# A transformer encoder layer on one core: the first stage written out in engine order, and half of a side product moved into it

## The chip, the cores and the metric

The kernel runs on one core of a Trainium2 chip. A core has five engines that each work through a list of instructions of their own, in order: TensorE (PE, matrix products; its weight loads are listed as PEld), VectorE (DVE), ScalarE (ACT), GpSimd (POOL) and SyncE (SP), which issues most of the transfers between the main memory and the core's own memory. They wait for one another through semaphores only. The metric is the device time of one execution in microseconds (us). Lower is better.

## The reference, cut to what matters

The layer normalizes 512 tokens of width 1024, projects them, runs two kinds of attention, adds a mixture of experts and a gated per-layer embedding. What the change touches:

```
h = layer_norm(x, emb_ln_g, emb_ln_b)                  # x: 512 x 1024
z = h @ w_in                                           # columns: NA q | NA k | NA v | c_q | c_kv | k_r
...
gate = jax.nn.sigmoid(h @ ple_gate_w[i] + ple_gate_b[i])
ple = gate * (p[i] @ ple_w[i])                         # p[i]: 512 x 256, ple_w[i]: 256 x 1024
```

`p[i] @ ple_w[i]` needs none of the layer's results, so it can be computed at any time before the gate.

## The kernel before, in words

Tokens are cut into four chunks of 128 (`h[0]` to `h[3]`, a chunk is 128 partitions x 1024). Most products are done in split precision: a float32 operand is cut into a high part (`...h`, a cast on ScalarE, line 94) and the remainder (`...l`, a subtraction on VectorE, line 95) by `split`, and `mm3` issues three products, high x high (L109), high x low (L110) and low x high (L111). Where operands are plain float32, one `nc.tensor.matmul` does the product.

**The first stage** (lines 260 to 279) is the program up to `v_na`, the NA v columns of `z`. For each chunk c, `layer_norm` runs on VectorE: two `bn_stats` of half a row each, `bn_aggr`, the variance plus epsilon `ve`; a square root `sd` on ScalarE; then `(h - mu) * eg`, five operations on 128 x 1 (the reciprocal, and `rsqrt_refine`), and `h * y + eb`. `eg` and `eb` are gain and bias, read once for each of the 128 partitions (`row_bcast`). `transpose_to` transposes the chunk on TensorE (eight 128 x 128 pieces into two `tr` tiles of PSUM) and splits the two tiles into `hTh`, `hTl`. Then eight steps of `mm3` (24 products of 128 x 512) sum up `pj`, and ScalarE copies it to `v_na`. The weight, columns 1024 to 1535 of `w_in`, comes in four pieces `raw` that are split into `aTh`, `aTl`. After the first stage come the latent projections (`latent_k`, weights by `in_cols`, columns from 1920), the attention, the output projection and the second normalization.

In this first stage the order of the instructions is not that of the code: the scheduler of the language orders each engine's list by its own estimates. The attention after it stands under `tc.manual_schedule` for TensorE, which keeps the order as written.

**The place of the side product** (lines 594 to 619) is after the attention. `pT` and `ple_w` are split, and for each of two halves hf of the columns and each chunk c, two steps of `mm3` (six products of 128 x 512) go to a tile `mm`, ScalarE copies it (`p_exp`, L618), and SP stores it to `ple_dram` (L619). It is read back much later, from line 986. The scheduler places these products among the normalizations `layer_norm(h[c], lg, lb, ...)` and transposes of the same stage. The routing projection with `w_q` follows (tiles `mm<-hTh,whi`, L109 to L111): its first two weights are each used in two passes of 256 tokens.

Of the kernel before, what the change touches and what calls it, by code (L numbers as in the profile page):

```python
# [9 lines left out]
F32 = mybir.dt.float32  # L10
# [5 lines left out]
OP = mybir.AluOpType  # L16
# [3 lines left out]
D = 1024  # L20
T = 512
# [49 lines left out]
def tile_encoder_layer(ctx: ExitStack, tc: tile.TileContext, A: dict, out: bass.AP):  # L71
# [97 lines left out]
    def ps_tile(name, bufs=2):  # L169
        return ps6.tile([128, 512], F32, name=name, bufs=bufs)  # L170
# [46 lines left out]
    def run_heads(kinds, feeds, at_unit):  # L217
# [32 lines left out]
        while step():  # L250
            pass

    aw = pA.enter_context(tc.tile_pool(name="aw", bufs=2, reuse_waits="tile"))
    p1 = ExitStack()
    iv = p1.enter_context(tc.tile_pool(name="iv", bufs=1, reuse_waits="tile"))
# [1 line left out]

    with tc.tile_pool(name="ln0", bufs=1, reuse_waits="tile") as ln0:  # L260
        nc.sync.dma_start(h[0], A["x"][0:128, :])
        eg = row_bcast(ln0, A["emb_ln_g"], "eg")
        eb = row_bcast(ln0, A["emb_ln_b"], "eb")
        for c in range(1, 4):
            nc.sync.dma_start(h[c], A["x"][c * 128:(c + 1) * 128, :])
        for c in range(4):
            layer_norm(h[c], eg, eb)
            transpose_to(hTh, hTl, h[c], c)
            if c == 0:
                for kk in range(4):  # L270
                    raw = wst.tile([128, 2, 512], F32, name="raw", bufs=3)
                    nc.sync.dma_start(raw, A["w_in"][kk * 256:(kk + 1) * 256, 1024:1536].rearrange(
                        "(k p) n -> p k n", p=128))
                    split(aTh[:, 2 * kk:2 * kk + 2], aTl[:, 2 * kk:2 * kk + 2], raw)
            cs = slice(c * 128, (c + 1) * 128)
            ps = ps_tile("pj")
            for k in range(8):
                mm3(ps, (hTh[:, k, cs], hTl[:, k, cs]), (aTh[:, k], aTl[:, k]), k == 0, k == 7)
            nc.scalar.copy(v_na[:, c, :], ps)

    ip = p1.enter_context(tc.tile_pool(name="ip", bufs=2, reuse_waits="tile"))
    v_sh = ip.tile([128, 3, 512], F32, name="v_sh", bufs=1)
# [7 lines left out]
    def in_cols(src, c0, ncols):  # L290

        return stream(src[:, c0:c0 + ncols].rearrange("(k p) n -> p k n", p=128), [8, ncols])

    def proj_steps(ps, w, m=128):
        for k in range(8):
# [10 lines left out]
    nc.sync.dma_start(gk, A["kg"])  # L306

    def latent_k(i, lat):
        w = in_cols(A["w_in"], 1920 + i * 128, 128)
# [279 lines left out]
    for c in range(4):  # L589
# [6 lines left out]
    ple_w = [stream(A["ple_w"][:, hf * 512:(hf + 1) * 512].rearrange("(k p) n -> p k n", p=128), [2, 512], scale=0.5)  # L596
             for hf in range(2)]
    for c in range(4):
        cs = slice(c * 128, (c + 1) * 128)
        ps = ps_tile("pj")  # L600
# [5 lines left out]
        transpose_to(hTh, hTl, h[c], c)  # L606


    for hf in range(2):
        hs = slice(hf * 512, (hf + 1) * 512)  # L610
        w = ple_w[hf]
        for c in range(4):
            cs = slice(c * 128, (c + 1) * 128)
            ps = ps_tile("mm")
            for k in range(2):
                mm3(ps, (pTh[:, k, cs], pTl[:, k, cs]), (w[0][:, k], w[1][:, k]), k == 0, k == 1)
            pl = aw.tile([128, 512], F32, name="p_exp", bufs=4)
            nc.scalar.copy(pl, ps)  # L618
            nc.sync.dma_start(ple_dram[c, :, hs], pl)  # L619
    p3.close()  # L620
    pA.close()

# [758 lines left out]
```

## Time and profile before

| what | value |
|---|---|
| three runs | 1562.61 to 1564.3 us, median 1564.05 us |
| the profiled execution, its own time | 1563.9 us |
| its span, from the first to the last instruction | 1562.1 us |
| PE busy | 1495.0 us (96%) |
| DVE busy | 1294.7 us (83%) |
| ACT busy | 647.3 us (41%) |
| transfers | 460.37 MB, mean 295 GB/s |

The share of busy time is a mean over the whole execution. The change touches the first 50 us and some 15 us around 310 us, so these two places are read by themselves, with the rows shown below.

### The profile page before, as it was taken

How to read it: one execution, taken by the hardware profiler on the slowest of the kernel's cores; microseconds unless marked ns; L12 is line 12 of the kernel's file. 1: busy time of each engine (PE TensorE's matmuls, PEld its weight loads, DVE VectorE, ACT ScalarE, POOL GpSimd, SP SyncE). 2: the span in 40 equal slices, each digit the busy share in tenths (PEclk: the TensorE clock that was granted, in tenths of full speed). 3: DMA queues.
4: the chain of work that ended last, by engine and by line, in shares of the span. 5: the costliest groups of instructions: out<-in, count | busy, mean ns of one | idle time of the engine just before them, and what ended most of it. 6: DMA issues, size and time to landing. Idle time of an engine off the chain costs nothing.

```text
span 1562.1 us, 22502 instructions
## 1 busy us (share of the span) xinstructions
PE 1495.0 (96%) x7715; PEld 1267.5 (81%) x7715; DVE 1294.7 (83%) x2895; ACT 647.3 (41%) x1171; POOL 559.6 (36%) x521
## 2 busy tenths in 40 slices
PE   6999899999999999999999989999899999999996
PEld 4788777788887889789888977888688888888885
DVE  7376795779989898988889938898688999998998
ACT  3265685333222566157424513333333333333332
POOL 1023110020015333443323346666434556655460
PEclk9999999999999999999999999999999999999998
DMA  7242341172239999999989999999999999999992
GB/s 232 64 115 80 90 122 42 57 257 81 73 130 356 326 390 391 397 409 419 416 316 374 388 386 354 403 398 392 361 397 377 377 398 397 401 395 398 382 335 110
DMA packets 189857, 460.37 MB, mean 295 GB/s; under 512 B 16560, under 2 KB 80432, under 8 KB 186672
## 3 DMA queue, kind: packets, MB, share of 16 engines
q1 hardware_dynamic: 121552, 213.55, 38.3%
q0 software_dynamic: 58400, 208.69, 35.2%
q10 hardware_dynamic: 9792, 36.70, 5.8%
q8 instruction: 61, 1.00, 0.3%
q14 instruction: 52, 0.43, 0.1%
HBM read 415.11 MB, written 40.89 MB: 292 GB/s over the span
## 4 chain that ended last, share of the span: by engine, by line
PE 70%; DMA 13%; DVE 12%; issue 3%; ACT 1%; POOL 0%; SPq 0%; ACTq 0%; DVEq 0%; POOLq 0%
PE acc L111 10%; PE acc L110 10%; PE acc L109 9%; PE mm L949 6%; PE hp L949 4%; DMA raw<-in_uT_dram 3%; PE mm L109 3%; PE tr L843 3%; PE mm L111 3%; PE pj L109 3%; PE mm L110 3%; PE pj L110 3%; PE pj L111 3%; DMA whi<-in_u_rows_dram,s_ix 3%; DMA wlo<-in_u_rows_dram,s_ix 2%
## 5 line engine op out<-in xcount | busy, mean ns | idle before, releaser
L949 PE MATMUL mm<-whole,raw 128*128 128x256 f32 x1120 | 252.0, 381 | 5.4 <-DMA raw<-in_uT_dram 4.9
L1167 POOL DMA_INDIRECT gat<-in_v_rows_dram,i_sel x128 | 194.4, 1519 | 154.3 <-DVE base L1169 124.8
L949 PEld LDWEIGHTS mm<-whole,raw 128*128 128x128 f32 x1120 | 209.8, 191 | 35.5 <-issue 4.4
L1152 POOL DMA_INDIRECT gat<-in_u_rows_dram,i_sel x97 | 147.1, 1516 | 110.6 <-DVE gat L1158 86.8
L109 PE MATMUL acc<-v_hi,a_hi 128*128 128x512 f32 x456 | 178.6, 392 | 6.1 <-ACT v_hi L94 6.1
L110 PE MATMUL acc<-v_lo,a_hi 128*128 128x512 f32 x456 | 178.7, 392 | 0.5 <-DVE v_lo L95 0.5
L111 PE MATMUL acc<-v_hi,a_lo 128*128 128x512 f32 x456 | 178.9, 393 | 0.1
L94 ACT CAST whi<-raw 128x1024 fp32r<-128x1024 f32 (+4 forms) x119 | 119.3, 1003 | 142.6 <-PE mm L110 41.0
L95 DVE TENSOR_TENSOR wlo<-raw,whi 128x1024 fp32r<-128x1024 f32 (+4 forms) x119 | 138.6, 1165 | 46.9 <-ACT whi L94 46.0
L1169 DVE SCALAR_TENSOR_TENSOR base<-gat,hdot,base 128x1024 f32<-128x1024 f32 x128 | 164.9, 1288 | 1.7
L94 ACT CAST v_hi<-v_raw 128x1024 fp32r<-128x1024 f32 x76 | 79.9, 1052 | 174.0 <-issue 88.7
L95 DVE TENSOR_TENSOR v_lo<-v_raw,v_hi 128x1024 fp32r<-128x1024 f32 x76 | 92.7, 1220 | 37.1 <-ACT v_hi L94 36.9
L110 PE MATMUL acc<-wlo,a_hi 128*128 128x512 f32 x312 | 121.6, 390 | 0.4 <-DVE wlo L95 0.4
L111 PE MATMUL acc<-whi,a_lo 128*128 128x512 f32 x312 | 121.5, 389 | 0.0
L1158 DVE SCALAR_TENSOR_TENSOR gat<-gat,h 128x1024 f32<-128x1024 f32 x97 | 114.7, 1222 | 8.1 <-DMA gat<-in_u_rows_dram,i_sel 8.1
L109 PE MATMUL acc<-whi,a_hi 128*128 128x512 f32 x312 | 121.3, 390 | 0.0
L894 POOL DMA_INDIRECT whi<-in_u_rows_dram,s_ix x43 | 44.9, 1044 | 211.2 <-DVE cand L747 133.1
L877 DVE TENSOR_SCALAR oh_j<-iota,eT 128x128 f32<-128x128 f32 x384 | 116.8, 379 | 0.0
L109 PEld LDWEIGHTS acc<-v_hi,a_hi 128*128 128x128 f32 x456 | 86.2, 189 | 23.9 <-ACT v_hi L94 6.6
L111 PEld LDWEIGHTS acc<-v_hi,a_lo 128*128 128x128 f32 x456 | 86.0, 189 | 18.8 <-DVE a_lo L95 1.0
L110 PEld LDWEIGHTS acc<-v_lo,a_hi 128*128 128x128 f32 x456 | 86.1, 189 | 18.5 <-DVE v_lo L95 1.0
L843 PEld LDWEIGHTS tr<-oh_i,oh_j 128*128 128x128 f32 x768 | 94.2, 193 | 7.7 <-ACT g_st L854 2.5
(364 smaller groups left out, 3355.4 us busy)
## 6 DMA issues: line engine op xcount, KB each, us to landing
raw<-in_uT_dram SPq DMA_DIRECT2D x116, 512.0 KB, 7.8
v_raw<-in_v_rows_dram SPq DMA_DIRECT2D x78, 512.0 KB, 12.9
raw<-in_v_rows_dram SPq DMA_DIRECT2D x50, 512.0 KB, 11.8
g_dram<-g_st ACTq DMA_DIRECT2D x24, 1024.0 KB, 8.8
ge_dram<-ge ACTq DMA_DIRECT2D x44, 256.0 KB, 7.2
ge<-ge_dram SPq DMA_DIRECT2D x44, 256.0 KB, 12.8
g_wide<-g_dram SPq DMA_DIRECT2D x9, 1024.0 KB, 17.9
raw<-in_w_in_dram SPq DMA_DIRECT2D x17, 512.0 KB, 4.0
```

Source lines behind the costliest of these rows:

```text
L94: nc.scalar.copy(hi, src)
L95: nc.vector.tensor_tensor(lo, src, r32(hi), op=OP.subtract)
L109: nc.tensor.matmul(ps, a[0], b[0], start=start, stop=False)
L110: nc.tensor.matmul(ps, a[0], b[1], start=False, stop=False)
L111: nc.tensor.matmul(ps, a[1], b[0], start=False, stop=stop)
L843: nc.tensor.matmul(ps[:, i * 128:(i + 1) * 128], oj[:, 4 * r + i, :], oi[:, 4 * r + i, :], start=True, stop=True)
L877: nc.vector.tensor_scalar(oj[:, i], iota, eT[:, 1, t0 + i:t0 + i + 1], eT[:, 2, t0 + i:t0 + i + 1], op0=OP.is_equal, op1=OP.mult)
L949: nc.tensor.matmul(ps[:, :N_U], raw[:, k], whole[:, k, :], start=(k == 0), stop=(k == 7))
L1152: nc.gpsimd.indirect_dma_start(out=u[:], out_offset=None, in_=u_rows, in_offset=bass.IndirectOffsetOnAxis(ap=i_sel[:, c, k:k + 1], axis=0))
L1158: nc.vector.scalar_tensor_tensor(u, u, 1.0, h[c], op0=OP.mult, op1=OP.mult, accum_out=hdot[:, c, k:k + 1])
L1167: nc.gpsimd.indirect_dma_start(out=u[:], out_offset=None, in_=v_rows, in_offset=bass.IndirectOffsetOnAxis(ap=i_sel[:, c, k:k + 1], axis=0))
L1169: nc.vector.scalar_tensor_tensor(base[c], u, hdot[:, c, k:k + 1], base[c], op0=OP.mult, op1=OP.add)
```

## The change

It has four parts.

1. The first stage stands under `tc.manual_schedule` for TensorE, VectorE and ScalarE: each of these lists now has the order in which the code emits. The pieces are generators that the code steps by hand (`norm_steps` in three parts, `v_steps` in eight steps and a copy).
2. The bias `eb` is no longer read once per partition. One row `b_row` is read, and two products with a column of ones (contraction over one partition) spread it over the partitions; ScalarE copies them.
3. The loads stand in the order of their use. The first latent weight `w_k` is loaded and split inside the first stage.
4. The first half (columns 0 to 511) of the side product is computed in the first stage, in plain float32: `ple_early`, two products of 128 x 512 for each chunk, a scaling copy on ScalarE, a store issued by GpSimd. At the old place only the second half is left.

```diff
-    with tc.tile_pool(name="ln0", bufs=1, reuse_waits="tile") as ln0:
+    with tc.tile_pool(name="ln0", bufs=1, reuse_waits="tile") as ln0, tc.manual_schedule(
+            engines={nc.tensor.engine, nc.vector.engine, nc.scalar.engine}):
         nc.sync.dma_start(h[0], A["x"][0:128, :])
+        b_row = ln0.tile([1, D], F32, name="b_row")
+        nc.sync.dma_start(b_row, ...)
         eg = row_bcast(ln0, A["emb_ln_g"], "eg")
-        eb = row_bcast(ln0, A["emb_ln_b"], "eb")
-        for c in range(1, 4):
+        eb = ln0.tile([128, D], F32, name="eb")
+        p_in = ln0.tile([128, 2, T], F32, name="p_in")
+        nc.sync.dma_start(p_in, A["pT"].rearrange("(k p) t -> p k t", p=128))
+        w_in0 = ln0.tile([128, 2, 512], F32, name="w_in0")
+        nc.sync.dma_start(w_in0, A["ple_w"][:, 0:512].rearrange("(k p) n -> p k n", p=128))
+        vraw = []
+        for kk in range(4):
+            vraw.append(...)
+            nc.sync.dma_start(vraw[kk], A["w_in"][kk * 256:(kk + 1) * 256, 1024:1536].rearrange(
+                "(k p) n -> p k n", p=128))
+            if kk == 2:
+                nc.sync.dma_start(h[1], A["x"][128:256, :])
+        for c in (2, 3):
             nc.sync.dma_start(h[c], A["x"][c * 128:(c + 1) * 128, :])
-        for c in range(4):
-            layer_norm(h[c], eg, eb)
-            transpose_to(hTh, hTl, h[c], c)
...
+        def norm_steps(r):
...
+            nc.scalar.sqrt(sd, ve)
+            yield
+            nc.vector.scalar_tensor_tensor(r, r, mu[:, 0:1], eg, op0=OP.subtract, op1=OP.mult)
...
+            rsqrt_refine(y, y0, ve, t)
+            yield
+            nc.vector.scalar_tensor_tensor(r, r, y, eb, op0=OP.mult, op1=OP.add)
+            yield
+        def ple_early(c):
+            ps = ps_tile("mm")
+            for k in range(2):
+                nc.tensor.matmul(ps, p_in[:, k, c * 128:(c + 1) * 128], w_in0[:, k], start=k == 0, stop=k == 1)
+            pl = aw.tile([128, 512], F32, name="p_t", bufs=4)
+            nc.scalar.mul(pl, ps, 0.5)
+            nc.gpsimd.dma_start(ple_dram[c, :, 0:512], pl)
...
+        go(norms[0], 2)
+        ple_early(0)
+        v_cut(0)
+        for x in turn(0):
+            split(*x)
+        ple_early(1)
+        v_cut(1)
+        go(sums[0], 4)
+        v_cut(2)
+        go(norms[1], 1)
+        v_cut(3)
+        go(sums[0], 5)
+        go(norms[1], 2)
+        ple_early(2)
+        t = turn(1)
+        ple_early(3)
+        for x in t:
+            split(*x)
+        go(norms[2], 3)
+        go(sums[1], 5)
+        t = turn(2)
+        go(sums[1], 4)
+        for x in t:
+            split(*x)
+        go(norms[3], 3)
+        w_k = [in_cols(A["w_in"], 1920, 128)]
+        go(sums[2], 5)
+        t = turn(3)
+        go(sums[2], 4)
...
-    for hf in range(2):
-        hs = slice(hf * 512, (hf + 1) * 512)
-        w = ple_w[hf]
-        for c in range(4):
...
+    for c in range(4):
+        cs = slice(c * 128, (c + 1) * 128)
+        ps = ps_tile("mm")
+        for k in range(2):
+            mm3(ps, (pTh[:, k, cs], pTl[:, k, cs]), (ple_w[0][:, k], ple_w[1][:, k]), k == 0, k == 1)
```

`turn(c)` issues the eight transposes of a chunk, and the `split` that follows cuts them; `v_cut(kk)` splits one piece of the weight.

**VectorE, first stage, before.** These are the rows of VectorE's list from the end of chunk 0's normalization on; `h_78`, `h_79` and `h_80` are chunks 1, 2 and 3, and `hTl` is the cut of a transposed chunk.

```order
L150 SCALAR_TENSOR_TENSOR h_77<-h_77,ln_y,eb 128x1024
L127 BN_STATS ln_st<-h_78 128x6 x2
L127 BN_STATS ln_st<-h_79 128x6
L128 BN_AGGR ln_mu<-ln_st 128x2
L127 BN_STATS ln_st<-h_79 128x6
L95 TENSOR_TENSOR hTl<-tr,hTh 128x4x128 x2
L129 TENSOR_SCALAR ln_ve<-ln_mu 128x1
L147 SCALAR_TENSOR_TENSOR h_78<-h_78,ln_mu,eg 128x1024
```

**VectorE, first stage, after.** These are the rows around the cut of chunk 1 (`tr_250`, `tr_255`), up to the cut of chunk 2 (`tr_305`).

```order
L305 SCALAR_TENSOR_TENSOR h_1_78<-h_1_78,ln_y_237,eb_124 128x1024
L95 TENSOR_TENSOR hTl_85<-tr_250,hTh_84 128x4x128
L95 TENSOR_TENSOR hTl_85<-tr_255,hTh_84 128x4x128
L290 BN_STATS ln_st_270<-h_2_79 128x6 x2
L292 BN_AGGR ln_mu_273<-ln_st_270 128x2
L294 TENSOR_SCALAR ln_ve_275<-ln_mu_273 128x1
L298 SCALAR_TENSOR_TENSOR h_2_79<-h_2_79,ln_mu_273,eg_122 128x1024
...
L305 SCALAR_TENSOR_TENSOR h_2_79<-h_2_79,ln_y_282,eb_124 128x1024
L95 TENSOR_TENSOR hTl_85<-tr_305,hTh_84 128x4x128
```

Before, the statistics of chunks 1 and 2 stand ahead of the cut of chunk 0; after, every operation of chunk 2's normalization stands between the cut of chunk 1 and the cut of chunk 2.

**ScalarE, first stage, after.** These are the rows from the last piece of the weight on; `p_t` is the copy of `ple_early`, `tr_250` belongs to chunk 1 and `tr_305` to chunk 2, and `pj_289` is the sum of chunk 1.

```order
L296 ACTIVATE ln_sd_217<-ln_ve_215 128x1
L94 CAST aTh_92<-raw4_136 128x1024
L336 COPY v_na_113<-pj_195 128x512
L313 ACTIVATE p_t_247<-mm_244 128x512
L313 ACTIVATE p_t_263<-mm_260 128x512
L94 CAST hTh_84<-tr_250 128x4x128
L94 CAST hTh_84<-tr_255 128x4x128
L296 ACTIVATE ln_sd_277<-ln_ve_275 128x1
L336 COPY v_na_113<-pj_289 128x512
L94 CAST hTh_84<-tr_305 128x4x128
```

The cut of chunk 1 now stands behind two copies of `ple_early`, and the cut of chunk 2 behind the copy of chunk 1's whole sum.

**TensorE, around 310 us, before.** These are the rows around the transposes of chunk 3 (`h_3_80`); `mm<-...,cqh` and `mm<-...,cql` are the side product, `mm<-hTh,whi` is the first product with `w_q`.

```order
L109 MATMUL mm_3262<-whi_2978,cqh_94 128x512
L194 MATMUL tr_3208<-ident_70,h_3_80 128x128 x4
L194 MATMUL tr_3215<-ident_70,h_3_80 128x128 x4
L110 MATMUL mm_3262<-wlo_2979,cqh_94 128x512
...
L111 MATMUL mm_3292<-whi_2978,cql_95 128x512
L109 MATMUL mm_3410<-hTh_84,whi_3406 128x256
```

**TensorE, the same place, after.**

```order
L111 MATMUL mm_3284<-whi_3010,cql_95 128x512
L194 MATMUL tr_3240<-ident_70,h_3_80 128x128 x4
L194 MATMUL tr_3247<-ident_70,h_3_80 128x128 x4
L109 MATMUL mm_3402<-hTh_84,whi_3398 128x256
L110 MATMUL mm_3402<-hTl_85,whi_3398 128x256
L111 MATMUL mm_3402<-hTh_84,wlo_3399 128x256
```

Before, 23 products of the side product stand between the transposes of chunk 3 and the first product with `w_q`; after, none does, and the 24 that are left all stand ahead of the transposes. Apart from these two places the lists of the engines are the same in both programs.

## Rows read from the trace of the kernel before

**Rows 1.** The page: chain that ended last, shares of the span by engine.

```profile
PE 70%; DMA 13%; DVE 12%; issue 3%; ACT 1%; POOL 0%; SPq 0%; ACTq 0%; DVEq 0%; POOLq 0%
```

**Rows 2.** Busy time by stretch: start:end us, length, then each engine's busy us (instructions).

```profile
8.00:32.00 24.00, 17.17 (x67) 12.98 (x68) 23.53 (x50) 9.44 (x15) 0.24 (x1) 1.00 0.85 277
32.00:46.30 14.30, 13.72 (x65) 10.62 (x64) 3.16 (x5) 3.10 (x6) 0.00 (x0) 1.00 0.27 57
```

**Rows 3.** Timeline, hand-over from chunk 2 to 3: start us, us, engine, line, operation.

```profile
32.45 1.08 ACT L94 CAST hTh<-tr 128x512 fp32r<-128x512 f32 x2
...
38.81 0.39 PE L111 MATMUL pj<-aTh,hTl 128*128 128x512 f32 x1
39.04 1.03 PE L194 MATMUL tr<-ident,h 128*128 128x128 f32 x8
39.24 0.59 ACT L279 COPY v_na<-pj 128x512 f32<-128x512 f32 x1 [5.70 <-PE pj L111]
39.72 1.08 ACT L94 CAST hTh<-tr 128x512 fp32r<-128x512 f32 x2
...
40.34 1.29 DVE L95 TENSOR_TENSOR hTl<-tr,hTh 128x512 fp32r<-128x512 f32 x2 [5.98 <-ACT hTh L94]
...
40.36 0.50 PE L109 MATMUL pj<-aTh,hTh 128*128 128x512 f32 x1 [0.29 <-ACT hTh L94]
...
46.31 0.39 PE L110 MATMUL pj<-hTl,whi 128*128 128x512 f32 x1
```

**Rows 4.** Timeline, TensorE: side product, chunk 3's transposes, first products with `w_q`.

```profile
309.45 1.07 PE L194 MATMUL tr<-ident,h 128*128 128x128 f32 x8
...
310.27 0.47 PE L110 MATMUL mm<-wlo,cqh 128*128 128x512 f32 x1
...
315.61 0.28 PE L109 MATMUL mm<-hTh,whi 128*128 128x256 f32 x1
...
319.23 0.39 PE L111 MATMUL mm<-hTh,wlo 128*128 128x256 f32 x1 [0.34 <-DVE wlo L95]
```

**Rows 5.** Timeline, VectorE: the normalization of chunk 0.

```profile
4.87 1.28 DVE L127 BATCH_NORM_STATS2 ln_st<-h 128x6 f32<-128x512 f32 x2 [3.82 <-DMA h<-in_x_dram]
...
6.43 0.15 DVE L129 TENSOR_SCALAR ln_ve<-ln_mu 128x1 f32<-128x1 f32 x1
7.03 1.28 DVE L147 SCALAR_TENSOR_TENSOR h<-h,ln_mu,eg 128x1024 f32<-128x1024 f32 x1 [0.45 <-DMA eg<-in_emb_ln_g_dram]
...
9.20 1.28 DVE L150 SCALAR_TENSOR_TENSOR h<-h,ln_y,eb 128x1024 f32<-128x1024 f32 x1
```

**Rows 6.** Timeline, TensorE: the first transposes, those of chunk 0.

```profile
10.63 1.94 PE L194 MATMUL tr<-ident,h 128*128 128x128 f32 x8 [10.63 <-DVE h L150]
```

**Rows 7.** Timeline, ScalarE: when the first and third piece of the weight landed.

```profile
15.18 1.04 ACT L94 CAST aTh<-raw 128x1024 fp32r<-128x1024 f32 x1 [0.74 <-DMA raw<-in_w_in_dram]
...
17.89 1.05 ACT L94 CAST aTh<-raw 128x1024 fp32r<-128x1024 f32 x1 [0.30 <-DMA raw<-in_w_in_dram]
```

**Rows 8.** Timeline, TensorE: a run of plain float32 products.

```profile
421.60 26.93 PE L949 MATMUL hp<-whole,early 128*128 128x256 f32 x124
```

**Rows 9.** Groups by form, 0 to 41 us: form, count, busy us, mean ns.

```profile
L95 DVE TENSOR_TENSOR aTl<-raw,aTh 128x1024 fp32r<-128x1024 f32 x4 | 4.9, 1222 | 0.2
L94 ACT CAST aTh<-raw 128x1024 fp32r<-128x1024 f32 x4 | 4.2, 1048 | 3.3 <-DMA raw<-in_w_in_dram 3.3
```

**Rows 10.** Timeline, TensorE: products after pauses; in brackets the idle time before.

```profile
176.28 0.47 PE L109 MATMUL pj<-cqh,whi 128*128 128x512 f32 x1 [2.49 <-DVE hTl L95]
...
824.52 1.23 PE L843 MATMUL tr<-oh_i,oh_j 128*128 128x128 f32 x8 [2.01 <-DVE oh_j L877]
826.68 1.89 PE L843 MATMUL tr<-oh_i,oh_j 128*128 128x128 f32 x8 [0.94 <-DVE oh_j L877]
```

**Rows 11.** Busy time by stretch; the number behind the brackets is TensorE's granted clock.

```profile
172.00:178.00 6.00, 3.51 (x16) 2.43 (x15) 4.12 (x9) 3.56 (x7) 3.91 (x8) 1.00 0.76 205
826.50:830.50 4.00, 3.81 (x14) 3.46 (x15) 4.00 (x13) 1.86 (x5) 1.88 (x2) 0.57 1.03 415
```

More of the change, by code (lines that the diff above doesn't have):

```diff
@@ L251, in run_heads, with in_cols @@
             pass
+    def in_cols(src, c0, ncols):
+        return stream(src[:, c0:c0 + ncols].rearrange("(k p) n -> p k n", p=128), [8, ncols])
     aw = pA.enter_context(tc.tile_pool(name="aw", bufs=2, reuse_waits="tile"))
@@ L256, in tile_encoder_layer @@
     v_na = iv.tile([128, 4, 512], F32, name="v_na")
-    with tc.tile_pool(name="ln0", bufs=1, reuse_waits="tile") as ln0:
+    with tc.tile_pool(name="ln0", bufs=1, reuse_waits="tile") as ln0, tc.manual_schedule(
+            engines={nc.tensor.engine, nc.vector.engine, nc.scalar.engine}):
         nc.sync.dma_start(h[0], A["x"][0:128, :])
+        b_row = ln0.tile([1, D], F32, name="b_row")
+        nc.sync.dma_start(b_row, bass.AP(tensor=A["emb_ln_b"].tensor, offset=A["emb_ln_b"].offset,
+                                         ap=[[0, 1], [1, D]]))
@@ L262, in tile_encoder_layer @@
         eg = row_bcast(ln0, A["emb_ln_g"], "eg")
-        eb = row_bcast(ln0, A["emb_ln_b"], "eb")
-        for c in range(1, 4):
-            nc.sync.dma_start(h[c], A["x"][c * 128:(c + 1) * 128, :])
-        for c in range(4):
-            layer_norm(h[c], eg, eb)
-            transpose_to(hTh, hTl, h[c], c)
[L269 to L274, printed above, removed]
+        eb = ln0.tile([128, D], F32, name="eb")
@@ new lines, in tile_encoder_layer @@
+        for c in (2, 3):
+            nc.sync.dma_start(h[c], A["x"][c * 128:(c + 1) * 128, :])
+        def norm_steps(r):
+            st = small.tile([128, 2, 6], F32, name="ln_st")
+            for i in range(2):
+                nc.vector.bn_stats(st[:, i, :], r[:, i * 512:(i + 1) * 512])
+            mu = small.tile([128, 2], F32, name="ln_mu")
+            nc.vector.bn_aggr(mu, st)
+            ve = small.tile([128, 1], F32, name="ln_ve")
+            nc.vector.tensor_scalar(ve, mu[:, 1:2], EPS, None, op0=OP.add)
+            sd = small.tile([128, 1], F32, name="ln_sd")
+            nc.scalar.sqrt(sd, ve)
+            yield
+            nc.vector.scalar_tensor_tensor(r, r, mu[:, 0:1], eg, op0=OP.subtract, op1=OP.mult)
+            y0 = small.tile([128, 1], F32, name="ln_y0")
+            nc.vector.reciprocal(y0, sd)
+            y = small.tile([128, 1], F32, name="ln_y")
+            t = small.tile([128, 1], F32, name="ln_t")
+            rsqrt_refine(y, y0, ve, t)
+            yield
+            nc.vector.scalar_tensor_tensor(r, r, y, eb, op0=OP.mult, op1=OP.add)
+            yield
@@ new lines, in ple_early, with turn @@
+        def ple_early(c):
[5 more added lines that the diff above has]
+            nc.gpsimd.dma_start(ple_dram[c, :, 0:512], pl)
+        def turn(c):
+            pss = []
+            for g in range(2):
+                ps = ps_tile("tr")
+                for i in range(4):
+                    d = 4 * g + i
+                    nc.tensor.transpose(ps[:, i * 128:(i + 1) * 128], h[c][:, d * 128:(d + 1) * 128], ident)
+                pss.append(ps)
+            return [(hTh[:, 4 * g:4 * g + 4, c * 128:(c + 1) * 128], hTl[:, 4 * g:4 * g + 4, c * 128:(c + 1) * 128],
+                     ps.rearrange("p (a b) -> p a b", b=128)) for g, ps in enumerate(pss)]
@@ L275, in tile_encoder_layer, with v_cut, v_steps @@
+        def v_cut(kk):
+            split(aTh[:, 2 * kk:2 * kk + 2], aTl[:, 2 * kk:2 * kk + 2], vraw[kk])
+        def v_steps(c):
             cs = slice(c * 128, (c + 1) * 128)
@@ L278, in tile_encoder_layer, with go @@
                 mm3(ps, (hTh[:, k, cs], hTl[:, k, cs]), (aTh[:, k], aTl[:, k]), k == 0, k == 7)
+                yield
             nc.scalar.copy(v_na[:, c, :], ps)
+            yield
+        def go(steps, n):
+            for _ in range(n):
+                next(steps)
+        norms = [norm_steps(h[c]) for c in range(4)]
+        sums = [v_steps(c) for c in range(4)]
+        for hf in range(2):
+            ps = psH.tile([128, 512], F32, name="hp")
+            nc.tensor.matmul(ps, ones[0:1], b_row[:, hf * 512:(hf + 1) * 512], start=True, stop=True)
+            if hf == 0:
+                go(norms[0], 1)
+            nc.scalar.copy(eb[:, hf * 512:(hf + 1) * 512], ps)
+        go(norms[0], 2)
[27 more added lines that the diff above has]
+        go(sums[2], 4)
+        for x in t:
+            split(*x)
+        w_k.append(in_cols(A["w_in"], 2048, 128))
+        go(sums[3], 9)
     ip = p1.enter_context(tc.tile_pool(name="ip", bufs=2, reuse_waits="tile"))
@@ L308, in latent_k @@
     def latent_k(i, lat):
-        w = in_cols(A["w_in"], 1920 + i * 128, 128)
+        w = w_k[i]
         ps = ps_tile("pj")
@@ L595, in tile_encoder_layer @@
     split(pTh, pTl, praw)
-    ple_w = [stream(A["ple_w"][:, hf * 512:(hf + 1) * 512].rearrange("(k p) n -> p k n", p=128), [2, 512], scale=0.5)
-             for hf in range(2)]
+    ple_w = stream(A["ple_w"][:, 512:1024].rearrange("(k p) n -> p k n", p=128), [2, 512], scale=0.5)
     for c in range(4):
@@ L606, in tile_encoder_layer @@
         transpose_to(hTh, hTl, h[c], c)
-    for hf in range(2):
-        hs = slice(hf * 512, (hf + 1) * 512)
-        w = ple_w[hf]
-        for c in range(4):
[L613 to L619, printed above, removed]
+    for c in range(4):
[3 more added lines that the diff above has]
+            mm3(ps, (pTh[:, k, cs], pTl[:, k, cs]), (ple_w[0][:, k], ple_w[1][:, k]), k == 0, k == 1)
+        pl = aw.tile([128, 512], F32, name="p_exp", bufs=4)
+        nc.scalar.copy(pl, ps)
+        nc.sync.dma_start(ple_dram[c, :, 512:1024], pl)
     p3.close()
```

4 lines of the change are left out of this document (2 added, 2 removed).

## The prediction, made before the changed kernel was run

> **What bounds the kernel now.** I read the page's chain first: of the work that ended last, 70% is TensorE's [rows 1], so time is won or lost where TensorE waits. Then I read the two places that the change touches, stretch by stretch. In the first stage VectorE is the bound until 32 us: it is busy 23.53 of 24 us, TensorE only 17.17 [rows 2]. From 32 us on TensorE is, with 13.72 of 14.3 us [rows 2]. By then all four chunks are normalized, since the scheduler filled VectorE's pauses with the statistics of later chunks. So a hand-over from one chunk to the next costs little: from the first `hTh` cast of chunk 2 (32.45) to that of chunk 3 (39.72) pass 7.27 us, and the stage's last chunk takes 6.59 us more, up to 46.31 [rows 3]. The reader is to see in those rows what follows what: last product of a sum, 0.43 us later the copy, 0.48 us later the first cast, 0.62 us later VectorE's cut, and TensorE starts the next sum with it. At the second place TensorE works without a pause through the transposes (309.45), 23 products of the side product (310.27 to 315.61) and into `w_q`, where it waits 0.34 us for a remainder [rows 4].
>
> **The first stage, order.** The lists show the decisive point. After the change, VectorE does the whole normalization of the next chunk only when it has cut the present one, and ScalarE casts the next chunk only when it has copied the present sum; that sum ends behind the next chunk's transposes. So each hand-over becomes one closed loop. Call a the first `hTh` cast of a chunk. VectorE's cut starts at a+0.62 and takes 1.29 [rows 3]: a+1.91. The normalization of the next chunk takes 1.71 up to the variance (4.87 to 6.58), 2.17 for the first wide operation and the five small ones (7.03 to 9.20; the root hides under the wide one) and 1.28 for the second [rows 5]: a+7.07. Transposes start 0.15 later, as chunk 0's did (10.48 to 10.63) [rows 5, 6], and take 0.82 until the next product (309.45 to 310.27) [rows 4]: a+8.04. Nine products are left of the present sum at 0.23 each (38.81 to 39.04) [rows 3], so the last starts at a+9.9; copy and cast follow by 0.43 and 0.48 [rows 3]: a+10.8. A loop is thus 10.8 us, not 7.27, and it is run twice (chunk 1 to 2, and 2 to 3). In it TensorE does 15 products from a+0.64 to about a+4.5, idles 2.7 us, does transposes and nine products, and idles 1.3 us.
>
> **The first stage, up to chunk 1.** The second full load, `eg`, was needed and landed at 7.03 [rows 5]; two pieces of the weight followed each other by 2.71/2 = 1.36 us per 512 KB [rows 7]. `w_in0` is now the fourth full load: 7.03 + 2 x 1.36 = 9.75. The weight's pieces become the fifth to seventh (11.1 to 13.8), `h[1]` the eighth (15.2), the last piece the ninth (16.5). TensorE's list has `ple_early(0)` ahead of chunk 0's transposes. 124 float32 products of 256 columns took 26.93 us, 0.217 each [rows 8], so 512 columns take 0.43; but the first transposes of the program ran at half pace, 1.94 us for eight [rows 6] against 1.03 later [rows 3], so I count 1.7 for two products here: 9.8 to 11.5. ScalarE then goes in written order: copy 0.6 (as the copy in [rows 3]) to 12.2, cast of piece 0 1.05 [rows 9] to 13.25, two casts of chunk 0 to 14.3, the copy of `ple_early(1)` (products done by 14.7) to 15.4, casts of pieces 1 and 2 to 17.5. VectorE follows with remainders of 1.22 [rows 9]: piece 2's ends at 18.95. Then come chunk 1's statistics to 20.7. The root, 0.2, stands ahead of the last piece's cast: cast to 22.0, remainder to 23.25. The rest of the normalization, 3.45, ends at 26.7; transposes to 27.7; `ple_early(3)` 0.86 to 28.6; its copy, ahead of the cast, to 29.4. So a is 29.4 for chunk 1, and 29.4 + 2 x 10.8 = 51.0 for chunk 3, where it was 39.72. The last chunk's 6.59 is unchanged. **First stage: +11.3 us.** The bounds are those of the landing: one load earlier or later, 1.4 either way, since everything hangs on `w_in0` in one chain.
>
> **Costs at nothing.** The spread bias: two cold products of 0.86 each after `b_row`, whose 4 KB stand ahead of `eg`, and two copies. `eb` is there by about 9.4 at the latest and is used at 9.20 [rows 5]; 0.2 us at most, covered by `ple_early(0)`, behind which chunk 0's transposes stand anyway. GpSimd's zeroing of the query tiles and its bias loads now stand behind four stores, the last of them issued at about 29; their first users come more than 10 us of latent products behind the stage's end. The first latent weight is cut during the idle stretches above, so the products after the stage do not wait more than before.
>
> **The second place.** 23 products go from behind the transposes: 315.61 - 310.27 = 5.34 us [rows 4]. The first `w_q` product then needs its weight cut earlier. ScalarE's list has that cast ahead of the last side copy, VectorE's remainder comes right after the normalization's end (309.30, 0.15 ahead of the transposes): 1.05 and 1.22 [rows 9] put the remainder at about 310.9, where the third product stands ready at 310.5. I count 0.3 lost: **-5.0 us**. Bounds: all 24 products, -5.6; or, if both weights' cuts came only behind the transposes, 2 x (1.05 + 1.22) = 4.5 of the 5.3 lost, -0.8. I stay near the upper one, since the lists and the loads allow it. What follows, up to the end, stands in the same lists as before and hangs on these products, so I let both terms run through to the end unchanged.
>
> **TensorE's clock.** The loops leave pauses of 2.7 and 1.3 us. After a pause of 2.49 us [rows 10] the granted clock stayed at 1.00, the 2.4 GHz level; around pauses of 2.01 and 0.94 us with transposes between them [rows 10] it was 0.57, mostly the 1.2 GHz level [rows 11]. One of two. A fall would make the 3.0 us of transposes and nine products up to twice as long. Two loops, half of them, half of that price: **+1.5 us**, bounds 0 and +6.
>
> The Trainium skill, "FP8 and Floating Point Precision", section "TensorE Precision Notes", says that true FP32 takes four passes through the array. The trace does not agree here: 0.217 us for 256 columns [rows 8] is less than the 0.23 of a split product of 512 [rows 3], so about two passes. By the page the sum would be nearer to +10.7.
>
> **Sum.** 11.3 + 1.5 - 5.0 = +7.8 us on the profiled execution's own 1563.9 us (span 1562.1 and 1.8 around it), 0.15 below the median of the runs: **1571.7 us, slower by 0.5%**. What a measurement of this kernel can tell from no change is about 0.2%, 3.1 us.
>
> **Rivals.**
> *Faster (other side).* The loop does not close: if VectorE were kept as busy as before, TensorE would again be the bound with 7.27 us a chunk, the stage would end near 46, and the 5.0 us would be all that counts: 1559. For it speaks that VectorE's work in the stage is hardly changed; against it the lists, which leave it nothing to do while it waits. It decides below a loop of 10.8 - (11.3 - 5.0)/2 = 7.65 us. 0.06.
> *No difference.* The chain to chunk 1, some twenty steps, is the least certain part. If loads land a place earlier and TensorE is at its upper level from the start, chunk 1 is cast near 26.5; with no clock loss and the full -5.6 the sum is about +2.8: 1566.7. 0.10.
> *The clock falls in each pause.* +6 in place of +1.5: 1576.2. For it the row with 0.57, against it the one with 1.00. 0.15.
> *The gain at the second place is lost* because the first `w_q` weights are cut late: 11.3 + 1.5 - 0.8: 1575.9. 0.08.
> *Float32 products cost four times a split product*, 0.93 instead of 0.43: at half pace `ple_early(0)` takes 3.6 instead of 1.7 and `ple_early(3)` 1.9 instead of 0.9, 2.9 more: 1574.6. Against it [rows 8]. 0.03. This is the rule of the page named above.
>
> **How the numbers follow.** My forecast, with its terms within their bounds, has 0.58; with the four others that end slower or level it makes 0.84 slower, 0.10 same, 0.06 faster. The range from 1567 to 1577 leaves out the faster case, half of the level one and the sum of several upper bounds.
>
> **What would show it.** Right: VectorE idle for 3 to 5 us ahead of the cuts of chunks 2 and 3, waiting for ScalarE's casts; TensorE waiting 2 to 3 us for chunks 2 and 3's second wide operation; first casts of chunks 1, 2 and 3 near 29, 40 and 51 us; the first product of the sum after chunk 3 at 57 to 60; from there to the first `w_q` product about 5 us less than before. Wrong: a distance of less than 8 us between the casts, `w_in0` needed later than 11 us, a pace of the products of 0.43 us behind the pauses, or a later stage that gives the delay back.

## The result and the profile after

The changed kernel takes 1570.97 us (median of 9 runs, 1568.62 to 1577.19), the kernel before 1564.3 us (9 runs beside them). The ratio is 1.0053, 95% interval 1.0038 to 1.0068: **slower by 0.5%**. The profiled execution took 1575.3 us (span 1573.5), 4.3 above the median of its kernel, so its two places are read one by one, and not its total.

The page's chain of work that ended last, which answers to [rows 1]: TensorE's share went from 70% to 77%.

```profile
PE 77%; DVE 9%; DMA 9%; issue 3%; ACT 2%; SPq 0%; DVEq 0%; ACTq 0%; POOLq 0%
```

Busy time by stretch, beside [rows 2] (columns as there: busy us and count of PE, PEld, DVE, ACT and POOL, then the granted clock, the busy share of the DMA engines and GB/s; the second stretch now reaches to the stage's new end):

```profile
8.00:32.00 24.00, 18.42 (x55) 10.35 (x54) 14.03 (x24) 7.89 (x12) 1.33 (x2) 0.93 0.81 281
32.00:62.30 30.30, 22.05 (x95) 15.40 (x94) 15.71 (x30) 6.98 (x13) 7.34 (x14) 1.00 0.31 83
```

VectorE, which was busy for 23.53 of the 24 us from 8 to 32, is now busy for 14.03: it waits for its turn in the list. The timeline of the first 35 us shows how late chunk 1 is. TensorE's rows first, then ScalarE's and VectorE's:

```profile
11.77 3.75 PE L311 MATMUL mm<-w_in,p_in 128*128 128x512 f32 x4 [2.88 <-DMA w_in<-in_ple_w_dram]
15.31 1.42 PE L322 MATMUL tr<-ident,h 128*128 128x128 f32 x8
...
28.83 2.34 PE L311 MATMUL mm<-w_in,p_in 128*128 128x512 f32 x4
31.01 1.04 PE L322 MATMUL tr<-ident,h 128*128 128x128 f32 x8
31.88 1.88 PE L311 MATMUL mm<-w_in,p_in 128*128 128x512 f32 x4
...
15.56 0.60 ACT L313 ACTIVATE p_t<-mm 128x512 f32<-128x512 f32 x1 [6.04 <-PE mm L311]
...
34.29 1.07 ACT L94 CAST hTh<-tr 128x512 fp32r<-128x512 f32 x2
...
8.88 1.28 DVE L298 SCALAR_TENSOR_TENSOR h<-h,ln_mu,eg 128x1024 f32<-128x1024 f32 x1 [2.31 <-DMA eg<-in_emb_ln_g_dram]
...
28.56 1.28 DVE L305 SCALAR_TENSOR_TENSOR h<-h,ln_y,eb 128x1024 f32<-128x1024 f32 x1
```

From there the loop that was foretold runs twice. The same timeline, from chunk 1's cut to the stage's end:

```profile
34.91 1.29 DVE L95 TENSOR_TENSOR hTl<-tr,hTh 128x512 fp32r<-128x512 f32 x2 [5.07 <-ACT hTh L94]
...
39.89 1.28 DVE L305 SCALAR_TENSOR_TENSOR h<-h,ln_y,eb 128x1024 f32<-128x1024 f32 x1
...
41.33 1.06 PE L322 MATMUL tr<-ident,h 128*128 128x128 f32 x8 [2.38 <-DVE h L305]
...
44.52 0.59 ACT L336 COPY v_na<-pj 128x512 f32<-128x512 f32 x1 [6.46 <-PE pj L111]
45.01 1.08 ACT L94 CAST hTh<-tr 128x512 fp32r<-128x512 f32 x2
...
45.65 0.50 PE L109 MATMUL pj<-aTh,hTh 128*128 128x512 f32 x1 [1.16 <-ACT hTh L94]
...
52.05 1.06 PE L322 MATMUL tr<-ident,h 128*128 128x128 f32 x8 [2.38 <-DVE h L305]
...
55.72 1.08 ACT L94 CAST hTh<-tr 128x512 fp32r<-128x512 f32 x2
...
62.29 0.40 PE L110 MATMUL pj<-hTl,whi 128*128 128x512 f32 x1
```

The casts stand at 34.29, 45.01 and 55.72: 10.7 us apart twice, where chunk 2's and 3's were 7.27 apart [rows 3]. The row that marked the stage's end before, at 46.31 (a latent product, 0.23 behind the stage's last one), stands at 62.29: **+16.0 us**.

The second place is read on TensorE's timeline, from the last product with `w2h` to the first with `w_q`. Before, it began here, 13.74 ahead of the first `w_q` product of [rows 4]:

```profile
301.87 0.39 PE L111 MATMUL pj<-w2h,aTl 128*128 128x512 f32 x1
```

After:

```profile
321.21 0.39 PE L111 MATMUL pj<-w2h,aTl 128*128 128x512 f32 x1
...
328.80 1.06 PE L194 MATMUL tr<-ident,h 128*128 128x128 f32 x8
329.61 0.37 PE L109 MATMUL mm<-hTh,whi 128*128 128x256 f32 x1
```

It takes 8.40 us now: **-5.3 us**. Together +10.6; the two profiled executions differ by 11.4, so all of the rest adds 0.8. That is a net figure: the attention of this execution took 3.0 us longer (last section), and the rest gives some 2 back.

### The profile page after: what moved, and what is told of

Same layout as the page of the kernel before. It is cut to its first block, busy times and chain, and to the rows that moved or that the text cites. A ratio compares the mean times of both kernels' runs of the same rounds, so it can differ in the third digit from the quotient of the medians.

```text
span 1573.5 us, 22500 instructions
## 1 busy us (share of the span) xinstructions
PE 1503.5 (96%) x7711; PEld 1266.2 (80%) x7711; DVE 1291.2 (82%) x2894; ACT 647.2 (41%) x1172; POOL 563.0 (36%) x525
## 4 chain that ended last, share of the span: by engine, by line
PE 77%; DVE 9%; DMA 9%; issue 3%; ACT 2%; SPq 0%; DVEq 0%; ACTq 0%; POOLq 0%
PE mm L1045 12%; PE acc L111 10%; PE acc L110 10%; PE acc L109 10%; PE tr L939 5%; DMA raw<-in_uT_dram 4%; PE hp L1045 4%; PE mm L109 3%; PE mm L111 3%; PE mm L110 3%; PE pj L109 3%; PE pj L110 3%; PE pj L111 3%; PE hp L111 1%; PE hp L109 1%
```

## The experiments

In each, the first stage is measured at the row that stood at 46.31 before, and the second place from the last product with `w2h` to the first with `w_q`, in one profiled execution. Us of a ratio are its excess over 1 times the median of the kernel before on that chip.

**1. Normalizations a chunk ahead.**

```
-        go(norms[2], 3)          (behind chunk 1's casts)
+        go(norms[2], 3)          (behind norms[1])
-        go(norms[3], 3)          (behind chunk 2's casts)
+        go(norms[3], 3)          (behind chunk 1's casts)
```

> The changed kernel with one thing moved: VectorE's list has the normalization of chunk 2 ahead of the cut of chunk 1, and that of chunk 3 ahead of the cut of chunk 2; TensorE's list and all loads are as in the changed kernel. Theory (the written order closes a loop through VectorE's normalization): VectorE does the normalization in the 5 us in which it waited for chunk 1's cast; TensorE no longer waits 2.4 us for chunks 2 and 3, the loop from cast to cast falls from 10.7 to about 8.1 us, the stage's last product comes about 5 us earlier (at about 57 instead of 62), the time falls by about 5 us against the changed kernel, to about 1566. Rival (late loads and the early side product alone make the loss): the casts stay 10.7 us apart or the gain is eaten ahead of the stage's end, 1571.

1.003 [1.0012, 1.0049], +4.7 us; the stage ends at 56.47, 5.8 earlier than in the changed kernel, 5.2 of it in the two loops (casts at 33.60, 41.72 and 49.88). TensorE's timeline has no wait ahead of chunk 2's transposes any more, only the one for the cast:

```profile
38.08 1.03 PE L322 MATMUL tr<-ident,h 128*128 128x128 f32 x8
...
42.37 0.50 PE L109 MATMUL pj<-aTh,hTh 128*128 128x512 f32 x1 [1.16 <-ACT hTh L94]
```

So half of the loop, VectorE's, is shown as a cause, with its price by the marks; the intervals of the two totals still overlap.

**2. The last product of a sum behind the next chunk's casts**, which opens the loop at ScalarE's end.

```
-        go(sums[1], 4)
+        go(sums[1], 3)
         for x in t:
             split(*x)
+        go(sums[1], 1)           (the same for sums[2])
```

> The changed kernel with ScalarE's list alone changed: the casts of chunks 2 and 3 stand ahead of the copies of chunks 1 and 2's sums. VectorE's list is as in the changed kernel. Theory: the loop loses the nine products, the copy and their hand-overs, 7.9 us from cast to cast instead of 10.7, so TensorE has no pause of 1.2 us ahead of each sum any more and the time falls by 5 to 6 us against the changed kernel, to about 1565.5. Rival (only VectorE's order matters): TensorE still waits 2.4 us for each normalization and no more than the 1.2 us per loop is won, 2.4 us in all, 1568.5.

1.0035 [1.0016, 1.0054], +5.5 us; the stage ends at 55.23, 7.1 earlier. Of this 2.6 lie ahead of chunk 1's cast (31.70 against 34.29), which this change of order does not touch; the two loops and what follows give 4.5. ScalarE's and TensorE's rows: the casts are 7.69 apart (10.72 in the changed kernel), the wait for VectorE is still there, the one for ScalarE is not.

```profile
31.70 1.07 ACT L94 CAST hTh<-tr 128x512 fp32r<-128x512 f32 x2
...
38.73 1.07 PE L322 MATMUL tr<-ident,h 128*128 128x128 f32 x8 [2.38 <-DVE h L305]
...
39.39 1.08 ACT L94 CAST hTh<-tr 128x512 fp32r<-128x512 f32 x2 [3.93 <-PE tr L322]
```

**3. No early product**: the side product whole in the second place, with the changed order in the first stage.

```
-        ple_early(0)             (and 1, 2, 3, with their two loads)
-    ple_w = stream(... 512:1024 ...)
+    ple_w = [stream(...) for hf in range(2)]
```

> The changed kernel without its fourth part: no early side product and no loads for it in the first stage, both halves at the old place. Theory: chunk 0's transposes no longer stand behind the side product (15.3 us), they start at about 11; the casts of chunk 1 lose two copies and two pairs of products and come at about 25.5 instead of 34.3; the two loops stay at 10.7; the stage ends near 53; the 5.3 us at the second place come back. In all about 3.5 us less than the changed kernel, 1567.5. Rival (the early side product lies in pauses and costs nothing): the stage ends at 62 as in the changed kernel and the time is 5 us more, 1576.

1.008 [1.0053, 1.0107], +12.5 us. The stage ends at 55.03 (7.3 earlier), the second place is as long as before (13.72). By the marks, the early products in this order cost more in the first stage than they give back in the second place, 7.3 against 5.3. The kernel should then be some 2 us faster than the changed one and is not; the intervals overlap, so the totals do not show it.

**4. Half of the side product left out**, in the kernel before.

> The kernel before, with its first stage untouched; of the side product only the second half is computed, and it is stored in both places (the first half of the product is left out). It measures what the second place is worth by itself. Theory (the 23 products behind chunk 3's transposes are on the path and nothing later gives it back): the first product with the routing weight starts 5.0 to 5.3 us earlier and the time falls by 5 us against the kernel before, to about 1559. Rival (a later stage that is bound by transfers takes it back): the first routing product comes 5 us earlier, but the time is that of the kernel before within 2 us.

0.9983 [0.9966, 1.0], -2.7 us: half of what was expected. The trace says why. The 23 products are gone, but the first `w_q` product now waits for VectorE, and the place takes 10.98 us, 2.8 less than before and not 5.3:

```profile
316.95 0.39 PE L109 MATMUL mm<-hTh,whi 128*128 128x256 f32 x1 [2.35 <-DVE hTl L95]
```

The order of the rows around it is the same as in the changed kernel. What differs is the wait of this one product: there it starts 0.81 behind the transposes without any, here it stands until VectorE has cut the first half of chunk 3.

**5. Both mended orders** (1 and 2 together).

> The changed kernel with both moves together: the normalizations of chunks 2 and 3 ahead of the cuts of chunks 1 and 2 on VectorE, and the casts of chunks 2 and 3 ahead of the copies of chunks 1 and 2's sums on ScalarE. Theory (one loop through both engines): with both opened TensorE alone sets the pace, 24 products and eight transposes, 6.5 to 7.3 us from cast to cast as in the kernel before; the stage ends about 8 us earlier than in the changed kernel, near 54.5, 8 us behind the kernel before; with 5.3 us won at the second place the time is about 1567, 0.1 to 0.2% above the kernel before. Rival (each move alone had taken what there was): the loops stay at 7.9 us and the stage ends near 56, as with one move.

1.0013 [0.9999, 1.0027], +2.0 us, the stage ends at 54.63, the second place takes 8.40. Three quarters of the loss are gone, and this interval lies wholly below that of the changed kernel.

**6. The early products of chunks 0 and 1 behind the fourth and the eighth step of sum 0**, to take the cold products out of the way of chunk 0's transposes.

```
-        ple_early(0)             (ahead of chunk 0's transposes)
-        ple_early(1)             (ahead of sum 0)
         go(sums[0], 4)
+        ple_early(0)
         ...
-        go(sums[0], 5)
+        go(sums[0], 4)
+        ple_early(1)
+        go(sums[0], 1)
```

> The changed kernel with the side products of chunks 0 and 1 moved behind the transposes of chunk 0 and into the sum of chunk 0, where TensorE waits for the weight's pieces; their copies stand later on ScalarE, too. Loads as in the changed kernel. Theory (chunk 0's transposes and casts stand queued behind the side product and its operand's load): chunk 0's transposes start at about 12.5 instead of 15.3, chunk 1's normalization ends at about 26 instead of 29.8, the stage about 3.5 us earlier than in the changed kernel, near 58.5; the time falls by 3.5 us against the changed kernel. Rival (the weight's pieces or the loads set the pace there, not the queue): chunk 0's transposes start early, but chunk 1's normalization ends within 1 us of 29.8.

A miss: 1.0136 [1.0113, 1.016], +21.3 us. Chunk 0's transposes came 4.3 earlier (11.00), and all of it was lost again, as the rival had it: chunk 1's second wide operation ended at 30.11, where it was 29.84.

```profile
18.00 1.88 PE L311 MATMUL mm<-w_in,p_in 128*128 128x512 f32 x4
21.49 0.50 PE L109 MATMUL pj<-aTh,hTh 128*128 128x512 f32 x1 [1.62 <-ACT aTh L94]
...
29.10 4.28 PE L311 MATMUL mm<-w_in,p_in 128*128 128x512 f32 x8
33.22 1.04 PE L322 MATMUL tr<-ident,h 128*128 128x128 f32 x8
...
19.91 0.60 ACT L313 ACTIVATE p_t<-mm 128x512 f32<-128x512 f32 x1 [5.38 <-PE mm L311]
20.40 1.04 ACT L94 CAST aTh<-raw 128x1024 fp32r<-128x1024 f32 x1
...
28.83 1.28 DVE L305 SCALAR_TENSOR_TENSOR h<-h,ln_y,eb 128x1024 f32<-128x1024 f32 x1
```

ScalarE waits 5.38 us for the moved product, and the weight's third cast stands behind its copy, so TensorE waits 1.62 for that. Two early products then stand together ahead of chunk 1's transposes, which start 3.1 us after their input is done. The clock has a share in it: it stood at 0.50 from 23.9 to 30.2, and in the first loop the nine products behind the transposes ran at half pace again (0.43 us apart), so that this loop took 12.3 us (casts at 36.51 and 48.80). The stage ends at 66.13. Behind it the second place takes 10.98 us, with the same wait as in run 4.

**7. The bias read instead of spread**: `row_bcast` for `eb`, no products with `ones`.

> The changed kernel without its second part: the bias is read for every partition behind the gain, as in the kernel before, and there is no row and no spreading product. Theory (the row is cheap, it saves a 512 KB load ahead of the side product's operands): the operands land 1.3 us later, the whole chain with them, the time is 1 to 1.5 us more than that of the changed kernel. Rival (the row of one partition, or what follows it, is what made the gain land at 8.9 us instead of 7.0): the gain lands at 7.0 as before, and the stage ends no later than in the changed kernel.

1.0064 [1.0046, 1.0083], +10.0 us: not to be told from the changed kernel. `eg` was needed at 7.46 there, `w_in0` at 11.60 (8.88 and 11.77 in the changed kernel), so `w_in0` did not come later with a full load in place of the 4 KB row, as I had expected. The stage ends at 60.85, 1.4 earlier; most of that is the clock (below). That the spread bias gains or loses anything is not shown.

**8. A filled order**: weight and `h[1]` ahead of the side product's loads, normalizations ahead, casts ahead of the last steps, each early product behind a sum.

```
+        t = turn(0)
+        v_cut(0)
+        go(norms[1], 1)
         ...
+        ple_early(0)
+        go(sums[0], 4)
         ...
+        t = turn(1)
+        go(sums[0], 2)
+        go(norms[2], 1)
```

> A version that should keep both gains: the changed kernel with written order, in which the load of chunk 1 stands behind the first piece of the weight and the side product's operands behind the second, each normalization is begun one chunk ahead, each cut stands ahead of the copy of the sum, and the side products fill places where TensorE waits. Theory: VectorE works nearly without a pause up to chunk 3's normalization, the stage ends near 50 to 52 us, 4 to 6 us behind the kernel before (four side products of two float32 passes' time each, 1.9 us, do not all fit into pauses); with 5.3 us won at the second place the time is that of the kernel before within 2 us, 1563 to 1566. Rival (float32 side products cost what they save wherever they stand): 1567 or more.

1.0015 [1.0001, 1.0028], +2.3 us. The stage ends at 53.05, the second place takes 11.01 (the wait of run 4). From 18.04 on TensorE waits once more in the stage, 2.03 us, so this order has little left to give.

**9. The early half alone**: the kernel before, whose scheduler places the four early products.

```
+        p_in, w_in0 = two loads behind the weight's
             nc.scalar.copy(v_na[:, c, :], ps)
+            ple_early(c)
-    for hf in range(2):          (second place: the second half only)
```

> The half of the side product in float32 alone: the first stage keeps the order of the kernel before (its scheduler places the four early products itself) and its bias load; only the two loads, the four products and the shorter second place are added. If the float32 products cost what they measured in the changed kernel (0.94 us each at the upper clock level, 7.5 us for the eight), and TensorE's pauses of the first stage take in a quarter of that, the stage ends 5 to 7 us later than before (52 to 54 us), the second place gives back 2.7 us (its first w_q product carries the wait for VectorE that also stands in the three runs with a gap of 11.0 us) and the sum is +2.5 to +4.5 us against before. Rival (the scheduler hides the products in the pauses, and the written order is the whole loss): stage end at 48 to 50 us, and the kernel within 1 us of before.

1.0007 [0.9983, 1.0031], +1.1 us. The stage ends at 51.60 and the second place takes 11.00. After the first two waits TensorE waits no more in the stage; the products stand between its other work:

```profile
15.48 0.80 PE L109 MATMUL pj<-aTh,hTh 128*128 128x512 f32 x1 [2.84 <-ACT aTh L94]
17.36 0.79 PE L110 MATMUL pj<-aTl,hTh 128*128 128x512 f32 x1 [1.09 <-DVE aTl L95]
...
23.98 1.88 PE L272 MATMUL mm<-w_in,p_in 128*128 128x512 f32 x4
...
51.60 0.39 PE L110 MATMUL pj<-hTl,whi 128*128 128x512 f32 x1
```

The stage ends 0.4 us below my range and 1.6 above the rival's: the products cost +5.3 there, so they are mostly not hidden. The ratio alone can't tell +2.5 from 0.

**10. Both mended orders without the early products.**

> Both mended orders (normalizations one chunk ahead, casts of a chunk before the last step of the sum ahead of it) without any early product: the side product stays whole in the second place. If order and product are the two parts of the loss and add up, the first stage ends 7.3 us earlier than with both orders and the product (55.1), so at 47 to 49 us against 46.8 before, the second place is as long as before (13.7 us), and the kernel stands at 0 to +2 us against before. Rival (the written order loses in itself, in the loads' order or the clock): stage end at 51 us or later, +4 us or more.

1.0028 [1.0013, 1.0044], +4.4 us; the stage ends at 51.62, later than expected. By stretch, the number behind the brackets is the granted clock:

```profile
11.70:22.70 11.00, 9.08 (x31) 6.60 (x32) 8.56 (x11) 4.20 (x6) 0.00 (x0) 1.00 1.00 321
22.70:36.30 13.60, 9.48 (x25) 6.42 (x24) 12.80 (x31) 1.95 (x5) 0.00 (x0) 0.50 0.06 13
36.30:52.00 15.70, 15.70 (x77) 12.96 (x76) 5.03 (x6) 5.63 (x9) 6.49 (x12) 1.00 0.46 118
```

For 13.6 us TensorE ran at 1.2 GHz. Not all of that cost time, since VectorE was busy for 12.80 of them and TensorE waited for it: 1.79 us ahead of chunk 1's transposes, and 2.03 for chunk 1's cut, which now stands behind chunk 2's normalization.

```profile
30.64 0.79 PE L111 MATMUL pj<-aTh,hTl 128*128 128x512 f32 x1 [2.03 <-DVE hTl L95]
```

From there to chunk 2's transposes (36.35) TensorE has no more waits; these 13 products took 5.7 us, and 3.1 in the changed kernel at the upper level. So an estimate of what the low clock cost is 2.6 us. Without it the stage would end near 49.0, still 2.7 behind the kernel before. Stage end and total are what the rival said (51 or later, +4 us or more): the written order, even mended, loses in itself.

**All runs together.** Sum of the two places, each against before (46.31 and 13.74), and what the whole kernel lost:

| run | stage end | second place | sum | measured, us |
|---|---|---|---|---|
| changed kernel | +16.0 | -5.3 | +10.6 | 8.3 [5.9, 10.6] |
| 1 normalizations ahead | +10.2 | -5.3 | +4.8 | 4.7 [1.9, 7.7] |
| 2 casts first | +8.9 | -5.3 | +3.6 | 5.5 [2.5, 8.5] |
| 3 no early product | +8.7 | 0.0 | +8.7 | 12.5 [8.3, 16.8] |
| 4 half left out | +0.3 | -2.8 | -2.5 | -2.7 [-5.3, 0.0] |
| 5 both orders | +8.3 | -5.3 | +3.0 | 2.0 [-0.2, 4.2] |
| 6 early products later | +19.8 | -2.8 | +17.1 | 21.3 [17.7, 25.0] |
| 7 bias read | +14.5 | -5.3 | +9.2 | 10.0 [7.2, 13.0] |
| 8 filled | +6.7 | -2.7 | +4.0 | 2.3 [0.2, 4.4] |
| 9 early half alone | +5.3 | -2.7 | +2.6 | 1.1 [-2.7, 4.9] |
| 10 orders only | +5.3 | 0.0 | +5.3 | 4.4 [2.0, 6.9] |

In ten of eleven the sum of the two lies in the interval, so within that width what the two places lose or gain runs through to the end. The marks contain the falls of the clock in their one execution: 1.0 us in the changed kernel's stage (below), 2.6 in run 10's. No complete kernel among them beats the one before.

## Why the prediction was right, and where its terms were not

The time, the sign and the mechanism were right. That 1571.7 lies 0.7 us from the median is partly luck: the sum of the terms was +7.8, the two places of the trace show +10.6, and the measured loss, 5.9 to 10.6, holds both. Two errors had opposite signs: the way up to chunk 1 was 4.9 too short, and the 1.5 for the clock did not come in the loops.

Of the signs that I had named, VectorE's idle time ahead of the cuts of chunks 2 and 3 (4.45 and 3.30) and TensorE's waits of 2.38 came. The three casts came 5 us late (34, 45 and 56 for 29, 40 and 51), and the end of the stage was late, too (62.3 for 57 to 60). `w_in0`, at 11.77, is past the 11 us that I had called a sign of being wrong. From the stage's end to the first `w_q` product it took 2.0 us less than before and not 5, since the attention took 3.0 longer.

**The closed loop: right.** 10.72 and 10.71 us for 10.8, twice; TensorE's pauses 2.38 and 1.16 for 2.7 and 1.3; the stage's tail (55.72 to 62.29) 6.57 for 6.59. Runs 1 and 2 each open one side of it and get 5.8 and 7.1 us back. The waits of the first 62 us name both sides:

```profile
DVE hTl L95 <- ACT hTh L94: 12.8, 3, 5.1
...
PE tr L322 <- DVE h L305: 4.8, 2, 2.4
PE pj L109 <- ACT hTh L94: 3.5, 3, 1.2
PE mm L311 <- DMA w_in<-in_ple_w_dram: 2.9, 1, 2.9
```

**Up to chunk 1: mis-sized by 4.9 us**, all of the stage's miss. I put chunk 1's cast at 29.4; it stands at 34.29. Chunk 1's second wide operation ended at 29.84, 3.1 later than I had it; the first two steps did that. The third is worth 1.0 and the fourth 0.7.
- *`w_in0` at 9.75*: it was needed at 11.77, +2.0 and outside my bound of 1.4 (10.81 to 11.28 in runs 1, 2 and 5, which have the same loads). I let the loads land one after another. The rate of the DMA engines in slices of 0.75 us says otherwise:

```profile
GB/s 0 0 142 311 295 147 191 216 325 330 377 352 393 401 393 412 404 399 391 404 410 393 410 347 295 167 205 294 355 229 178 269 311 361 293 311 328 92 44 18
```

 The first 15 slices (11.25 us) add up to 2.9 MB, while the four full loads up to `w_in0` are 2.1 MB. The other 0.8 MB can only be of loads issued behind it; at some 390 GB/s they are worth an estimated 2.1 us. This is read from bytes; no run changed it alone.
- *Float32 products at 1.7 for the first two and 0.86 later*: they are twice as long. The first two start at 11.77 and their copy at 15.56, where I had 11.5: +4.0, 2.0 of it the landing. At the upper level two take 1.88. I had divided [rows 8] by 124, but the trace keeps two records for one such product: in the kernel `ple_early` is two products, in the rows it is x4, so the run of 124 records is 62 products. So it is 0.43 for 256 columns. For 512 it is 0.94 busy, and 0.86 from start to start: in run 9 two of them and one split product took 1.94 us (23.98 to 25.92). That is nearly four times a split product's 0.23 [rows 3]. The rule of the Trainium skill, "FP8 and Floating Point Precision", section "TensorE Precision Notes" (four passes for true FP32), agrees with that, and my sentence that the trace does not agree was wrong. The rival built on it had 0.03 and 2.9 us; its mechanism is what happened.
- *The clock ahead of the loops, which I had at the upper level*: `ple_early(2)` stands ahead of chunk 1's transposes. The clock fell before it (window below), and it ran until 31.0, 1.0 longer than the transposes' input needed. Run 7 has the same rows there and no fall; in it the product was done in time, and the transposes waited for VectorE:

```profile
29.51 1.06 PE L319 MATMUL tr<-ident,h 128*128 128x128 f32 x8 [0.31 <-DVE h L302]
```

 Chunk 1's cast stands at 32.82 there, 1.5 earlier; 0.5 of that it had gained before.
- *`ple_early(3)` at 0.86*: it is twice as long, too, and its copy stands ahead of the cast.

**The second place: right.** -5.3 for -5.0; the 0.3 that I took off for a wait did not come. That a wait there can take half of it is shown by the four runs at 11.0 (4, 6, 8, 9), as the rival with the lost gain had it, though for chunk 3's remainder and not for the weight.

**The clock: +1.5 did not come where I put it.** In the loops it stayed up; it fell once before them, for 3.4 us, and cost the 1.0 us above. In run 6 it did fall in a loop, behind the same wait of 2.38, and that loop took 1.6 us more than the other; the term was possible, and did not occur here. Windows of the changed kernel, the clock behind the brackets:

```profile
26.30:29.70 3.40, 3.17 (x7) 2.17 (x8) 3.23 (x8) 0.59 (x1) 0.00 (x0) 0.51 0.58 173
29.70:62.00 32.30, 24.05 (x104) 16.72 (x103) 15.85 (x31) 7.58 (x14) 7.34 (x14) 1.00 0.29 77
```

**What the change is worth, part by part.** Run 9 against before: the early half alone, +5.3 in the stage and -2.7 to -5.3 in the second place, about nothing or a small loss. Run 3 against before: the written order without it, +8.7 in the stage and 12.5 [8.3, 16.8] in all. Run 9 against the changed kernel: the written order with its loads, +10.7 in the stage. So the order is nearly the whole loss. Run 7: the spread bias, nothing that can be told. Runs 5 and 8 get most of the order's loss back and still only come near the kernel before. One reason can be worked out: eight float32 products at 0.86 are 6.9 us, the 24 split ones that they replace 5.5 at 0.23.

**Open.** Why the first `w_q` product has the later wait in four kernels was not found; no run changed it alone. Why runs 3 and 6 lie high against the sum of their two places was not followed either. Over all executions their granted clock was 0.985 and 0.983 in the mean, and 0.988 in the kernel before beside them; but run 10 was low, too (0.983 against 0.987), and lies within its interval.

## What to carry to other kernels

Before writing an engine order by hand, follow one chunk around: if the next chunk's first operation stands behind the present chunk's last on each of two engines, the stage runs at the length of that loop, whatever the engines' busy shares say. Work moved into another stage's pauses must be priced there, in its new precision, and a row's count must be compared with the program's list before dividing by it. Two marks in the trace, ahead of and behind each place that is touched, say where each of eleven kernels loses its time, where several totals cannot be told apart.

## What was not expected of the hardware

One float32 product of 128x128 by 512 columns took 0.94 us busy at the upper clock level, 0.86 from start to start, and left two records.

The granted clock differed where TensorE's list did not. Run 7 has the same pauses in sum 0 (1.11 and 0.76 us) as the changed kernel, 0.5 us earlier, and no fall:

```profile
23.00:28.00 5.00, 3.14 (x11) 1.81 (x11) 3.59 (x10) 1.61 (x3) 0.00 (x0) 1.00 0.97 291
28.00:36.00 8.00, 6.53 (x25) 3.50 (x24) 3.86 (x7) 2.27 (x5) 3.12 (x6) 1.00 0.20 73
```

In the attention, behind a pause of 2.47 us in the changed kernel and 2.48 us in run 2, at the same product, the clock was 0.76 in the one (first row) and 1.00 in the other:

```profile
190.00:197.00 7.00, 4.68 (x15) 3.62 (x16) 4.31 (x9) 2.61 (x6) 3.40 (x7) 0.76 0.93 229
```

```profile
182.50:189.50 7.00, 4.52 (x25) 3.63 (x24) 4.75 (x10) 3.75 (x10) 3.87 (x8) 1.00 0.84 205
```

So the length of a pause does not decide whether the clock falls, and the clock can be worth 3.0 us in one stretch: from the first scores of the second kind of attention to the output projection the changed kernel took 50.6 us at a granted clock of 0.93, run 2 and the kernel before 47.7 and 47.6 at 1.00. The total follows: of the nine executions of the changed kernel the two with a mean clock of 0.990 took 1568.6 and 1569.0 us, the two with 0.986 took 1577.1 and 1577.2.
